# Hybrid trunk layer: the last tile's stash in the context's place, its second pass begun in the scan, outs and gates in separate places, and w_ada issued in turn

## The chip, the cores and the metric

The kernel runs on one core of one Trainium2 chip. The metric is the device time of one execution in microseconds (us), lower is better. The core has five engines with a queue of instructions each: PE (TensorE, matmuls; the loading of its weights is listed as PEld), DVE (VectorE), ACT (ScalarE), POOL (GpSimd) and SP (SyncE, which here only issues DMA transfers). An engine takes its instructions strictly in order.

## The reference

One layer on 2048 latent tokens and 256 context tokens of width 1024, batch 1. The part around the change is the mixer, a gated linear recurrence with 8 heads of 128 in two directions:

```python
m_l = (sc_lat @ w_ada[l] + b_ada[l])[:, None, :]     # sc_lat = silu(c); six vectors of 1024
hl = modulate(rmsnorm(lat, norm_g[l, 0]), sh1, sc1)
q, zf_fwd, zf_bwd, v, g = split(hl @ w_in)
S_t = diag(f_t) S_{t-1} + k_t v_t^T,  o_t = S_t^T q_t     # per head, forward and backward
y = (rmsnorm(o_fwd + o_bwd, g_gain) * silu(g)) @ w_out
lat = lat + g1 * y
hl = modulate(rmsnorm(lat, norm_g[l, 1]), sh2, sc2)
lat = lat + g2 * conv_ffn(hl, w_up, conv_w, conv_b, w_down)
return rmsnorm(lat, final_g)
```

## The kernel before, in words

The 2048 tokens are 16 tiles of 128, numbered 0 to 15 (NT = 16), in two groups of 8 and units of 4. Products are made of operands split in two parts (`split`, L76 to L78: ACT rounds, DVE subtracts), with three matmuls for high-high, high-low and low-high.

**Head (L186 to L230).** The first two of the six modulation vectors come from 16 tiles of `w_ada`, 128x1024 each (512 KB). All 16 transfers are issued first (L199), eight on ACT's queue and eight on SP's; then ACT does the sigmoid (L201), DVE the product (L202), and TensorE 64 matmul passes into `mps` (L208). The x tiles of the first norms are loaded behind (`early_x`).

**Scan (`mixer_scan`, L269 to L736).** For each group and head the projections (L332 to L334) and the forward and backward recurrence in chunks. Work is put on an agenda: `at(clock + n, f)` runs f n ticks later, one tick per step of the projections, and this sets the order of the code. What the backward state from later tiles must still add is kept for a second pass: for each tile, per head, the summed k v products, the decayed q, the outputs o so far and the gates g go to DRAM (`stash`), all but the last head of tile 15, which stays in `late`, inside the tile Sf. In the last head of the second group `out_weight` loads and scales w_out (L634, L635) and splits it into the `wo` places; rows 4 to 7 are held in the context's place (tag cxt) and split after the scan.

**Second pass (`mixer_out`, L877 to L1095).** From tile 15 down to 0: `heads(t)` multiplies the running state Sb with the tile's q (L908), adds o (L912), squares on ACT (L915), updates Sb (L917), sums the squares (L920), makes 1/rms on POOL (L74) and scales o (L925 on DVE, L927 on ACT). `heads_T` transposes o (L937), multiplies with the gate (L939) and splits into ghl (L77, L78). `residual` has 24 matmuls for each half of the row (L948 to L950) and adds to lat (L953). The norm of the tile above follows (`norm_steps`, L955 to L962; `norm2`, transposes at L109), and sums of its transposes are stored for the FFN (L974). The kq and og loads (L889) go over SP; each has two places, for even and odd tiles, and og holds outs and gates in one place that one load fills. The gate product is written over the gates. Code order is `heads` two tiles ahead, `heads_T` one ahead, inside the first `residual`.

The order of instructions on each engine comes from the code's order and a scheduler that works on it; a place of a pool is given again when its last reader is done. Transfers take one of eight semaphore lanes in turn, so that one waits for the eighth before it.

The FFN follows (L1234 and on), untouched but for shifts of time.

## Time and profile before

| what | us |
|---|---|
| median of 3 runs (2834.51 to 2838.2) | 2835.72 |
| the profiled execution | 2833.49 |
| its span | 2831.8 |
| TensorE busy | 2735.7 |
| w_ada's matmuls, start and length | 15.21, 29.49 |
| the scan's last matmul, start | 1270.78 |
| second pass, first matmul | 1280.98 |

The span is the time between the first and the last instruction recorded; the little that is missing to the execution's time lies around it. Rows of a timeline give start, duration, engine, line, operation, output and inputs, and in brackets how long the engine had been idle and what ended this. In a busy row, matmuls are pipelined: their modelled ends lie past the next one's start.

### The profile page before, as it was taken

The page shows a single profiled execution, that of the slowest core. Times are in us where ns is not written, and L with a number is a line of the kernel's source. Part 1 is how long each engine was busy: PE and PEld are TensorE (multiplying, and loading weights), DVE is VectorE, ACT ScalarE, POOL GpSimd, SP SyncE. Part 2 cuts the span into 40 slices and gives each one's busy share as a digit, 9 for nine tenths or more (in the row PEclk, how much of TensorE's full clock was granted, in tenths as well). Part 3 has the DMA queues.
Part 4 walks back from the last instruction along what each step waited for, and adds up shares of the span by engine and source line. Part 5 has one row for each costly group of instructions (what it writes and reads, how often), then busy time and mean ns, then how long its engine had stood idle before and what let it go on. Part 6 is the DMA issues. An engine that isn't in the chain of part 4 may idle for free.

```text
span 2831.8 us, 41982 instructions
## 1 busy us (share of the span) xinstructions
PE 2735.7 (97%) x16072; PEld 2267.8 (80%) x16072; DVE 1978.9 (70%) x2804; ACT 1149.9 (41%) x1910; POOL 563.6 (20%) x882
## 2 busy tenths in 40 slices
PE   6899999999999999998898899999999999999998
PEld 2688888888888888886777788888888888887887
DVE  3555556657565765667787788777878777576887
ACT  4523443333333333334556444444444444333343
POOL 2211111111111111111110343333444332000001
PEclk9899999999999999999999999999999999999999
DMA  5122332224542442226778522226422223987663
GB/s 223 34 68 83 109 112 84 93 60 153 179 127 72 128 125 80 91 76 224 253 276 288 209 90 90 68 81 217 155 89 90 90 71 113 310 305 252 191 201 123
DMA packets 223777, 402.18 MB, mean 142 GB/s; under 512 B 29012, under 2 KB 136404, under 8 KB 217816
## 3 DMA queue, kind: packets, MB, share of 16 engines
q1 hardware_dynamic: 219544, 390.78, 41.6%
q10 hardware_dynamic: 4032, 8.72, 0.8%
q8 instruction: 126, 2.06, 0.3%
q14 instruction: 75, 0.61, 0.1%
HBM read 289.04 MB, written 110.38 MB: 141 GB/s over the span
## 4 chain that ended last, share of the span: by engine, by line
PE 67%; DMA 7%; DVE 6%; issue 1%; ACT 1%; POOL 1%; SPq 0%; DVEq 0%; ACTq 0%; POOLq 0%
PE z L332 8%; PE z L334 8%; PE z L333 7%; PE y L1395 3%; PE y L1393 3%; PE y L1394 3%; PE zc L790 3%; PE zd L790 3%; PE zd L793 3%; PE zc L793 3%; PE zd L792 3%; PE zc L792 3%; PE za L793 3%; PE za L790 3%; PE za L792 3%; PE kv L536 1%
## 5 line engine op out<-in xcount | busy, mean ns | idle before, releaser
L332 PE MATMUL z<-tok,w 128*128 128x512 f32 x1280 | 516.3, 404 | 0.0
L334 PE MATMUL z<-tok,w 128*128 128x512 f32 x1280 | 503.1, 393 | 0.0
L333 PE MATMUL z<-tok,w 128*128 128x512 f32 x1280 | 501.6, 392 | 0.0
L78 DVE TENSOR_TENSOR w<-raw,w 128x512 fp32r<-128x512 f32 (+1 forms) x260 | 239.4, 925 | 144.6 <-ACT w L77 140.7
L334 PEld LDWEIGHTS z<-tok,w 128*128 128x128 f32 x1280 | 241.5, 189 | 51.2
L332 PEld LDWEIGHTS z<-tok,w 128*128 128x128 f32 x1280 | 242.5, 190 | 47.5 <-issue 3.5
L333 PEld LDWEIGHTS z<-tok,w 128*128 128x128 f32 x1280 | 242.1, 189 | 44.7
L77 ACT ACTIVATE w<-raw 128x512 fp32r<-128x512 f32 (+1 forms) x260 | 195.7, 759 | 131.3 <-PE zd L793 77.1
L1395 PE MATMUL y<-wd,ml 128*128 128x512 f32 x600 | 234.0, 390 | 2.6 <-DVE ml L78 2.6
L1393 PE MATMUL y<-wd,mh 128*128 128x512 f32 x600 | 233.7, 389 | 0.7 <-ACT X L1428 0.7
L1394 PE MATMUL y<-wd,mh 128*128 128x512 f32 x600 | 233.5, 389 | 0.0
L386 DVE TENSOR_TENSOR_SCAN S<-F,d 128x528 f32<-128x528 f32 (+1 forms) x80 | 91.6, 1145 | 99.8 <-ACT F L369 99.2
L78 DVE TENSOR_TENSOR w<-s,w 128x512 fp32r<-128x512 f32 x126 | 121.3, 967 | 52.5 <-ACT w L77 51.7
L790 PE MATMUL zc<-rT,w 128*128 128x512 f32 x352 | 137.1, 390 | 1.2 <-DVE uv L1280 1.0
L793 PE MATMUL zc<-rT,w 128*128 128x512 f32 x352 | 136.9, 389 | 0.0
L792 PE MATMUL zc<-rT,w 128*128 128x512 f32 x352 | 136.9, 389 | 0.0
L1395 PEld LDWEIGHTS y<-wd,ml 128*128 128x128 f32 x600 | 112.6, 188 | 27.8 <-DVE ml L78 4.5
L77 ACT ACTIVATE w<-s 128x512 fp32r<-128x512 f32 x126 | 78.2, 627 | 137.3 <-POOL s L846 80.6
L1393 PEld LDWEIGHTS y<-wd,mh 128*128 128x128 f32 x600 | 112.6, 188 | 24.8 <-ACT X L1428 1.2
L1394 PEld LDWEIGHTS y<-wd,mh 128*128 128x128 f32 x600 | 112.6, 188 | 23.3
L790 PE MATMUL za<-rB,w 128*128 128x512 f32 x336 | 130.7, 389 | 0.0
L792 PE MATMUL za<-rB,w 128*128 128x512 f32 x336 | 130.7, 389 | 0.0
(323 smaller groups left out, 6220.1 us busy)
## 6 DMA issues: line engine op xcount, KB each, us to landing
raw<-in_w_up_dram SPq DMA_DIRECT2D x88, 512.0 KB, 4.1
raw<-in_w_in_dram SPq DMA_DIRECT2D x80, 512.0 KB, 3.8
lr<-m SPq DMA_DIRECT2D x49, 512.0 KB, 5.5
m<-r SPq DMA_DIRECT2D x66, 256.0 KB, 4.1
spare<-in_w_ada_dram SPq DMA_DIRECT2D x32, 512.0 KB, 4.9
kq<-stash SPq DMA_DIRECT2D x15, 1024.0 KB, 5.6
og<-stash SPq DMA_DIRECT2D x15, 1024.0 KB, 6.0
u<-in_w_down_dram SPq DMA_DIRECT2D x51, 256.0 KB, 4.0
```

Of the source, the lines that this page charges most:

```text
L77: act.activation(h, src, AF.Copy)
L78: dve.tensor_tensor(l, src, h.bitcast(F32), OP.subtract)
L332: pe.matmul(z, w[:, 0, k], h, start=k == 0, stop=False, skip_group_check=True)
L333: pe.matmul(z, w[:, 0, k], l, start=False, stop=False, skip_group_check=True)
L334: pe.matmul(z, w[:, 1, k], h, start=False, stop=k == KT - 1, skip_group_check=True)
L386: dve.tensor_tensor_scan(flat(S[:, d]), flat(F[:, d]), flat(d1[:, 0:ns]), 0.0, OP.mult, OP.max)
L790: pe.matmul(o, w[:, 0, k], r[:, :, 0, k], start=start and k == 0, stop=False, skip_group_check=True)
L792: pe.matmul(o, w[:, 0, k], r[:, :, 1, k], start=False, stop=False, skip_group_check=True)
L793: pe.matmul(o, w[:, 1, k], r[:, :, 0, k], start=False, stop=k == 3, skip_group_check=True)
L1393: pe.matmul(z, lh, rh, start=start, stop=False, skip_group_check=True)
L1394: pe.matmul(z, lh, rl, start=False, stop=False, skip_group_check=True)
L1395: pe.matmul(z, ll, rh, start=False, stop=stop, skip_group_check=True)
```

## The change

The stash gets the layout [128, 4, 8, 128], one plane each for k v, q, o and g. Three things are done.

**In the head**, the sigmoid and its product stand before the loop over k, and each k issues its two w_ada transfers and its matmuls; the x tiles are issued after k = 3, 4 and 5.

**At the end of the scan**, tile 15's stash for heads 0 to 6 is loaded into the context's place (`load_top`, 12 ticks into the last head), and the last head's four planes are copied there directly. Its head step (`last_heads`) is put beside the last unit's output gate, and its transposes and gate product (`last_turn`) right after the scan, into places of Sf and raw. Rows 4 to 7 of w_out now use the ring of the w_in weights, and all rows are asked for in another order (4 to 7, then 0 to 3, a tick apart). The steps that finish the last head's units come earlier.

**In the second pass**, outs and gates have a place and a load of their own, both issued in `turn` behind the transposes; the gate product is written to PSUM and split from there. `heads(14)` stands in tile 15's first residual half, `heads(13)` behind it, tile 15's `turn` after its second half, the other turns after k = 1 in place of 3, and the load of `conv` after tile 15.

```diff
-        for n, wt in enumerate(wts):
-            (sp if n % 2 else act).dma_start(
-                wt, a["w_ada"][n // 2 * 128:(n // 2 + 1) * 128, n % 2 * D:(n % 2 + 1) * D])
         act.activation(sil, vec[:, V_C:V_C + 16], AF.Sigmoid)
         dve.tensor_tensor(sil, sil, vec[:, V_C:V_C + 16], OP.mult)
-        for t in range(-2, 1):
-            early_x(t)
         for k in range(KT):
             for i in range(2):
+                n = 2 * k + i
+                wt = ada[n // 4][:, n % 4]
+                (sp if i else act).dma_start(
+                    wt, a["w_ada"][k * 128:(k + 1) * 128, i * D:(i + 1) * D])
...
+            if 3 <= k < 6:
+                early_x(k - 5)
...
+        def load_top():
+            tops.append(hq.tile([128, 4, NH, 128], F32, name="top", tag="cxt", bufs=1))
+            sp.dma_start(tops[0][:, :, 0:NH - 1], stash[NT - 1][:, :, 0:NH - 1])
...
+        def last_heads():
+            heads_core(tops[0], tops[0][:, 2], NT - 1,
+                       lambda: ps.tile([128, 4, 128], F32, name="oi", tag=banks.pop(0), bufs=1),
+                       lambda n: gp.tile([128, NH], F32, name=n, tag=n, bufs=1))
...
-            query(1, 14)
-            value(0, (5, 9, 13))
-            if g == 1 and h == NH - 1:
-                value(1, (9, 13, 17))
+            query(1, 13 if last else 14)
+            value(0, (4, 7, 10) if last else (5, 9, 13))
+            if last:
+                value(1, (3, 5, 7))
+                at(clock[0] + 9, last_heads)
                 out_gate(0)
-                for k in range(4):
-                    at(clock[0] + 2 * k, lambda k=k: out_weight(k))
+                weight(4)
+                for n, k in enumerate((4, 5, 6, 7, 0, 1, 2, 3)):
+                    at(clock[0] + n, lambda k=k: out_weight(k))
...
         run(1 << 30)
+        last_turn()
         for k in range(4, KT):
...
-    ogs2 = qp.tile([128, 2, NH, 2, 128], F32, name="og", tag="og", bufs=1)
+    ogs2 = qp.tile([128, 2, 2, NH, 128], F32, name="og", tag="og", bufs=1)
...
-                g = og[:, hs, 1]
-                dve.tensor_tensor(g, tp, g, OP.mult)
-                split(gh[:, hs], gl[:, hs], g)
+            dve.tensor_tensor(tp, tp, g_[:, hs], OP.mult)
+            split(gh[:, hs], gl[:, hs], tp)
...
         def turn():
-            gs.append(heads_T(t - 1, ogs.pop(0)))
+            gs.append(heads_T(t - 1))
+            if t > 1:
+                load_stash(3, 1, t - 2)
+            if t > 2:
+                load_stash(2, 1, t - 3)
...
-            residual(0, lat, *g, between=turn if 0 < t < NT - 1 else None)
             if t == NT - 1:
-                turn()
-            if t > 2:
-                gts[t - 3] = load_stash(1, t - 3)
+                residual(0, lat, *g, between={3: lambda: heads(t - 1)})
+                heads(t - 2)
+            else:
+                residual(0, lat, *g, between={1: turn} if t else {})
```

What stands in order on three engines, before and after. First ACT at the program's start (wada are the tiles of w_ada, sil the sigmoid, x_ the first token tiles). Before:

```order
L199 DMA wada<-in_w_ada_dram 128x1024 x8
L201 ACT_TABLE_LOAD
L201 ACTIVATE sil<-vec 128x16
L97 ACTIVATE junk,ss<-x_168 128x1024
L100 ACTIVATE x_168<-x_168,rs 128x1024
```

After:

```order
L202 DMA wada<-in_w_ada_dram 128x1024 x2
L196 ACT_TABLE_LOAD
L196 ACTIVATE sil<-vec 128x16
L202 DMA wada<-in_w_ada_dram 128x1024 x4
L97 ACTIVATE junk,ss<-x_176 128x1024
L202 DMA wada<-in_w_ada_dram 128x1024
L100 ACTIVATE x_176<-x_176,rs 128x1024
```

The sigmoid now has two transfers ahead of it in place of eight, and the others stand between it and the norms' squares.

Next DVE where the scan ends and the second pass begins (wo are the split parts of w_out, raw, spare and wraw its rows; L374, L414 are the scan's last gate). Before:

```order
L78 TENSOR_TENSOR wo<-raw,wo 128x1024
L78 TENSOR_TENSOR wo<-spare,wo 128x1024
L78 TENSOR_TENSOR wo<-raw,wo 128x1024
L374 TENSOR_TENSOR g<-z,g 128x512
L78 TENSOR_TENSOR wo<-spare,wo 128x1024 x3
L917 SCALAR_TENSOR_TENSOR Sb<-Sb,decb,kq 128x128 x5
L912 TENSOR_TENSOR og<-og,oi 128x4x128
L917 SCALAR_TENSOR_TENSOR Sb<-Sb,decb,kq 128x128
L912 TENSOR_TENSOR og<-og,oi 128x4x128
L917 SCALAR_TENSOR_TENSOR Sb<-Sb,decb,kq 128x128 x2
L920 TENSOR_REDUCE ss_11971<-oi 128x4 x2
```

After, from the sums of tile 15's squares on (L289 to L294 are the lines that stood at L920 to L925, L304 stood at L939, L677 at L635; top is tile 15's stash):

```order
L289 TENSOR_REDUCE ss_11826<-oi 128x4 x2
L78 TENSOR_TENSOR wo<-raw,wo 128x1024
L73 TENSOR_SCALAR rs_11827<-ss_11826 128x8
L677 SCALAR_TENSOR_TENSOR raw<-raw,vec,g_11234 128x1024
L294 TENSOR_TENSOR top<-top,rs_11827 128x512
L414 TENSOR_TENSOR g<-z,g 128x512
L78 TENSOR_TENSOR wo<-wraw,wo 128x1024
L78 TENSOR_TENSOR wo<-raw,wo 128x1024
L677 SCALAR_TENSOR_TENSOR raw<-raw,vec,g_11234 128x1024
L304 TENSOR_TENSOR tp<-tp,top 128x512 x2
L78 TENSOR_TENSOR wo<-raw,wo 128x1024
L78 TENSOR_TENSOR gl<-tp,gh 128x512 x2
```

Before, all pieces of w_out are split before the first instruction of tile 15; now the head step of tile 15 stands ahead of most of them, and its gate product (L304) and split (gl) among them. On TensorE the eight matmuls of tile 15's head step now have the last 21 matmuls of the scan's gate behind them, then come its transposes, 29 matmuls of the residual, and the eight of tile 14's head step, with the 19 that are left of tile 15's two halves behind them.

Last SP inside the second pass, from the kq load of one tile on (stash_79 is tile 15's, stash_73 tile 9's). Before, from an og load to the second next store of lat:

```order
L889 DMA og<-stash_75 128x2048
L1059 DMA lat_94<-lat 128x1024
L974 DMA rhs1T_11914<-w 128x1024
L889 DMA kq<-stash_73 128x2048
L1019 DMA lat<-in_x_dram 128x1024
L889 DMA og<-stash_74 128x2048
L1059 DMA lat_93<-lat 128x1024
```

After:

```order
L1044 DMA lat<-in_x_dram 128x1024
L949 DMA kq<-stash_73 128x2048
L949 DMA og<-stash_74 128x1024
L1091 DMA lat_93<-lat 128x1024
L949 DMA og<-stash_73 128x1024
L1003 DMA rhs1T_11968<-w 128x1024
```

One og load of 128x2048 has become two of 128x1024: gates (those of tile 10, stash_74) come behind the kq of tile 9, and outs (those of tile 9, stash_73) behind the store of lat.

## The prediction

> **What bounds the kernel now.** First the page: its span, and how busy each engine is.

> ```profile
> span 2831.8 us, 41982 instructions
> ...
> PE 2735.7 (97%) x16072; PEld 2267.8 (80%) x16072; DVE 1978.9 (70%) x2804; ACT 1149.9 (41%) x1910; POOL 563.6 (20%) x882
> ```

> TensorE is the bound; no matmul is removed by this change, so all that can go is its idle time, or its time at a low clock. The profiled execution took 2833.49 us for a span of 2831.8; the median of the three runs shown is 2835.72, 2.2 above it. I make the sum against 2833.5 and add 2.2 at the end. A measurement of this kernel can tell about 0.2% (5.7 us) from no change.

> Next the waits of TensorE (us in total, times, longest), to see what the idle time is:

> ```profile
> PE mps L208 <- DVE sil L202: 15.2, 1, 15.2
> PE y L948 <- DVE lat L953: 13.4, 7, 4.6
> ...
> PE tp L109 <- DVE xn L962: 8.5, 7, 2.1
> ```

> Then the busy time by stretch (PE, PEld, DVE, ACT, POOL; then the granted clock, DMA share, GB/s):

> ```profile
> 200.00:1263.00 1063.00, 1059.63 (x8255) 898.72 (x8254) 675.54 (x976) 357.67 (x608) 162.59 (x398) 1.00 0.33 103
> ...
> 1322.00:1516.30 194.30, 177.29 (x962) 148.86 (x961) 153.16 (x324) 109.95 (x256) 25.98 (x24) 1.00 0.73 256
> ```

> The scan is full (1059.6 of 1063), so nothing is to be won inside it. The reader should see three holes, and each has one part of the change on it: the first 15.2 us, the handover from scan to second pass (rows below), and the second pass (17.0 us of 194.3).

> **Head: w_ada issued in turn.** The timeline of the first microseconds (start, duration, engine, line):

> ```profile
> 0.81 12.60 ACTq L199 DMA_DIRECT2D wada<-in_w_ada_dram  x8
> ...
> 4.26 0.17 DVE L243 TENSOR_TENSOR lbw<-vec 128x16 f32<-128x16 f32 x1 [4.26 <-DMA vec<-in_vecs_dram]
> ...
> 13.44 1.28 ACT L201 ACT_TABLE_LOAD   x1 [13.44 <-DMA wada<-in_w_ada_dram]
> 14.73 0.22 ACT L201 ACTIVATE sil<-vec 128x16 f32<-128x16 f32 x1
> 14.98 0.18 DVE L202 TENSOR_TENSOR sil<-sil,vec 128x16 f32<-128x16 f32 x1 [3.46 <-ACT sil L201]
> ...
> 15.21 29.49 PE L208 MATMUL mps<-wada,sil 128*2 128x512 f32 x64 [15.21 <-DVE sil L202]
> ```

> The sigmoid needs only vec, which is there at 4.26, but it stands on ACT behind eight DMA issues that take until 13.44. Afterwards two issues stand ahead of it. Its table load needs no data, so it can run before 4.26; sigmoid 0.22, product 0.18 and two hops of 0.05 to 0.25 put TensorE's start at about 5.0, or at 5.9 if the table load waits for vec: I take 5.3. Then the weights must keep up:

> ```profile
> GB/s 0 159 365 385 396 412 421 412 418 412 412 407 415 410 404 412 407 423 410 421 407 407 112 0 243 265 246 251 44 0 11 0 0 0 0 0 0 96 377 333
> ```

> The forty slices of 0 to 60 us show some 410 GB/s, so a 512 KB tile each 1.28 us, 2.56 us for the two of one k; TensorE spends 29.49/8 = 3.7 us on a k. It isn't starved. The DMA burst, x tiles and first raws included, ends in slice 22 (33 us), before the matmuls would (5.3 + 29.5 = 34.8). So the whole start moves by 15.2 − 5.3 = **9.9 us** (8 to 10.5); what follows to 200 us hangs on these sums and moves along.

> **Handover.** TensorE's timeline, from the scan's last matmul to the first transposes of norm2:

> ```profile
> 1270.78 0.39 PE L562 MATMUL o<-v,at 128*128 128x128 f32 x2
> 1280.98 3.78 PE L908 MATMUL oi<-Sb,kq 128*128 128x128 f32 x16 [9.80 <-DMA kq<-stash]
> 1288.55 3.56 PE L908 MATMUL oi<-Sb,kq 128*128 128x128 f32 x16 [3.80 <-DVE ss L920]
> ...
> 1294.55 0.50 PE L948 MATMUL y<-wo,ghl 128*128 128x512 f32 x1 [1.22 <-ACT ghl L77]
> ...
> 1308.49 1.95 PE L908 MATMUL oi<-Sb,kq 128*128 128x128 f32 x16
> 1310.19 0.48 PE L948 MATMUL y<-wo,ghl 128*128 128x512 f32 x1
> ...
> 1313.01 1.04 PE L937 MATMUL tp<-ident,og 128*128 128x128 f32 x8
> ...
> 1321.87 0.39 PE L950 MATMUL y<-wo,ghl 128*128 128x512 f32 x1
> 1322.10 1.03 PE L109 MATMUL tp<-ident,xn 128*128 128x128 f32 x8
> ```

> From 1271.17 to 1322.10 are 50.9 us. In them lie four head groups (from 1308.49 to the next start at 1310.19: 1.7 each, since a modelled end overlaps the next start by 0.25), three transpose groups (1.04, so 0.8) and 96 matmuls of the residual (the last at 1321.87, 0.23 before the next): 31.3 us. So 19.6 are lost: the gaps of 9.80, 3.80 and 1.22, and half speed around them.

> The change takes away the wait for the load of tile 15, but puts its head group in front of the last 21 gate matmuls (4.8 us) and tile 15's whole readout behind them, on DVE. Prices of the operations, by groups (busy, mean ns, idle before) and then from DVE's timeline:

> ```profile
> L912 DVE TENSOR_TENSOR og<-og,oi 128x512 f32<-128x512 f32 x32 | 21.3, 683 | 24.5 <-DMA og<-stash 24.5
> ...
> L920 DVE TENSOR_REDUCE ss<-oi 128x4 f32<-128x512 f32 x32 | 20.5, 682 | 0.0
> ...
> L939 DVE TENSOR_TENSOR og<-tp,og 128x512 f32<-128x512 f32 x32 | 21.8, 684 | 3.6 <-PE tp L937 3.6
> ...
> L77 ACT ACTIVATE ghl<-og 128x512 fp32r<-128x512 f32 x32 | 19.2, 621 | 9.6 <-DVE og L939 9.6
> ...
> L74 POOL TENSOR_TENSOR rs<-rs,mhalf 128x8 f32<-128x8 f32 x16 | 26.4, 1650 | 88.1 <-DVE rs L73 88.1
> ```

> ```profile
> 1270.53 1.29 DVE L635 SCALAR_TENSOR_TENSOR raw<-raw,vec,g 128x1024 f32<-128x1024 f32 x1 [1.32 <-DMA raw<-in_w_out_dram]
> 1271.73 1.22 DVE L78 TENSOR_TENSOR wo<-raw,wo 128x1024 fp32r<-128x1024 f32 x1
> ...
> 1292.10 1.13 DVE L917 SCALAR_TENSOR_TENSOR Sb<-Sb,decb,kq 128x128 f32<-128x128 f32 x4
> ```

> By the order on DVE: two adds 1.4, eight Sb updates 2.1 (four take 1.13), two sums 1.3, a wo split 1.2, the power on POOL 1.7 with its hops 0.4, the scaling 0.7: 8.8 from the head group to the transposes, less 4.8 of cover: **4.0 idle**. Between transposes and the first residual matmul stand a last piece of the scan's gate 0.7, two wo splits 2.4, a scaling of raw 1.3, the gate multiplication 0.7 and ACT's rounding 0.6: 5.7, less 0.8 beside the transposes and 0.7 because DVE's instructions begin up to 0.1 before the one ahead ends (the split at 1271.73 behind the scaling that lasts to 1271.82): **4.2**, then 0.8 for gl. Half clock behind that is 2.5 (the tail below shows such a stretch). Head group 14 has the same chain without the split and with some overlap, 7.2, over 19 matmuls (4.3): 2.9. The two lat additions, the next gate product and rounding: 2.7; half clock after these gaps 2.5. Sum 19.6 against 19.6 lost: **gain 0**. Bounds: 7 better if the weight splits slip behind the chain, 6 worse if raw for k = 3 lands late, since its scaling stands in this chain:

> ```profile
> raw<-in_w_out_dram SPq DMA_DIRECT2D x2, 512.0 KB, 5.1
> ```

> It can be issued only when the split ahead frees its place, and the work between is about 5.9 us: enough cover for 5.1 and an issue, nothing to spare.

> How long a gap brings half speed these rows bound: behind the tail's 4.59 (below) the matmuls come at half rate, and in front of the gap of 3.80 the head groups were slow already (3.78 against 1.95 later).

> [...]

> **Second pass, tiles 13 to 2.** Six pairs of tiles run from 1322.10 to the row of 1516.31 below: 194.2/6 = 32.4 us a pair, with 177.29/6 = 29.5 of matmuls. What delays them starts at DVE, as its waits in 1296 to 1560 us show:

> ```profile
> DVE og L912 <- DMA og<-stash: 22.5, 9, 3.6
> DVE og L925 <- POOL rs L74: 18.5, 15, 1.5
> ```

> The timeline of one tile (its transposes, then the load into its place), and SP's waits, show what holds the loads:

> ```profile
> 1395.57 1.03 PE L937 MATMUL tp<-ident,og 128*128 128x128 f32 x8
> ...
> 1407.85 0.32 SPq L889 DMA_DIRECT2D og<-stash  x1
> ```

> ```profile
> SPq L889 <- DVE ghl L78: 78.2, 14, 7.9
> ```

> DVE waits up to 3.6 us for outs of the next tile, since one load brings outs and gates into one place, and SP can't issue it before the last ghl split of the tile whose place it takes has read the product there. In order behind that wait stand xn and lat, and TensorE waits for those. With places apart, outs come free with the transposes, and the product goes to PSUM, so gates come free one multiplication later, not after two splits (L939 reads PSUM at 684 ns, L912 and L920 cost the same; the splits of a product in PSUM are taken at that price). By the order the outs' load is issued right after those transposes: near 1396.6 in place of 1407.85, 11 us earlier, where it comes 3.6 late at most. DVE then has 153.16/6 = 25.5 of work a pair and 2 x 1.23 of waits for POOL: 28 to 29, under TensorE's 29.5. I take 29.9 a pair: 6 x 2.5 = **15 us** (6 to 17: the upper end is all of TensorE's idle, the lower leaves two waits in three). The extra DMA issue per tile on SP (0.3 us) is covered by SP's waits of the row above.

> **Tail.**

> ```profile
> 1516.31 1.06 PE L109 MATMUL tp<-ident,xn 128*128 128x128 f32 x8 [0.67 <-DVE xn L962]
> 1521.96 0.77 PE L948 MATMUL y<-wo,ghl 128*128 128x512 f32 x1 [4.59 <-DVE lat L953]
> ...
> 1527.22 1.27 PE L937 MATMUL tp<-ident,og 128*128 128x128 f32 x8
> ```

> The gap of 4.59 is the same DVE chain, with nothing else for TensorE; the 12 matmuls after it take 5.26 us to 1527.22, 0.44 each where 0.23 is full speed: 2.5 lost. With DVE some 2 us ahead, as without a wait of 3.6 at most behind it, the gap is 2.4 and the clock stays up: 2.2 + 2.5, taken as **4** (0 to 7).

> **Sum.** −9.9 + 0 − 15 − 4 = −29; 2833.5 − 29 = 2804.5; with 2.2 it is **2807**.

> **Rivals.** A: the handover really closes: TensorE finds the chain of tile 15 nearly done, since the wo splits slip behind it or beside the scan. For it: DVE has 4.2 us of splits in the chain that nothing there needs. Against: they stand in DVE's order. It saves up to 13 of the 19.6 more: 2794.

> B: the second pass only trades its wait: DVE has just 0.8 us of slack a pair, and rhs stores, lat and kq loads share the 0.73 of DMA. Then head and a little remain: 2833.5 − 9.9 − 1 + 2.2 = 2825. The edit would be done, and not do what it says for the outs.

> C, slower: SP is one queue in order, now with four loads a tile, and an outs load that waits for transposes stands ahead of the kq load and of the rhs stores whose buffers DVE needs. If that makes each of 14 tiles 1.3 us later: 2833.5 + 18.2 − 9.9 + 2.2 = 2844. It decides from 9.9/14 = 0.7 us a tile. Against it: the 78.2 us that SP already waits for the splits, most of which go.

> D: the clock falls in both new gaps of the handover. Eight transposes and up to 12 matmuls more go at half rate, 0.9 to 2.5 more: about 2809. [...]

> **Chances.** Forecast 0.58, A 0.14, B 0.17, D 0.06, C 0.05. The range takes the forecast with its unknowns (handover, pairs), A and D and the nearer side of B: 2792 to 2823. Faster by over 0.2% (under 2830) are all but C and the far side of B: 0.92; within 0.03; slower 0.05.

> **What would show it.** Head: the mps group starts near 5 and lasts 29.5; later than 7, and the sigmoid still waited. Handover: no wait for kq; instead two waits of about 4 us, for the scaled outs and for the gate product; a wait of DVE for raw means the load was late. Second pass: the outs' wait for the stash falls from 22.5 to a few us, and the starts of the norm2 transposes lie under 30.5 apart; if they lie at 32, B holds. Tail: the 4.59 halves. Wrong would be above all a DVE whose waits move to rhs buffers or kq at the same length.

## The result, and the profile after

The changed kernel takes 2798.89 us (median of 4 runs, 2796.79 to 2800.06) against 2835.11 before (4 runs, 2834.23 to 2838.2): a ratio of 0.9869, 95% interval 0.9852 to 0.9887, so 36 us faster where 29 were forecast. The page of its profiled execution:

```profile
span 2797.0 us, 42007 instructions
...
PE 2732.9 (98%) x16072; PEld 2269.1 (81%) x16072; DVE 1977.5 (71%) x2804; ACT 1147.7 (41%) x1908; POOL 571.9 (20%) x882
```

The span is 34.8 us shorter. The waits of TensorE, as shown of before (us in total, times, longest):

```profile
PE mps L205 <- DVE sil L197: 5.2, 1, 5.2
PE y L977 <- ACT gh L77: 3.8, 1, 3.8
...
PE tp L303 <- ACT top L296: 3.5, 1, 3.5
...
PE tp L303 <- DVE og L294: 3.2, 2, 1.8
...
PE y L977 <- ACT ghl L77: 1.8, 1, 1.8
...
PE tp L109 <- DVE xn L991: 0.5, 1, 0.5
```

The wait for lat (13.4 us in 7 places), that for kq (9.8) and that for xn in the second pass are gone; new are those of 3.5, 3.8 and three of under 2 in the handover. The twelve tiles of the second pass, by stretch (PE, PEld, DVE, ACT, POOL, clock, DMA share, GB/s):

```profile
1312.40:1486.20 173.80, 173.80 (x961) 149.45 (x960) 154.89 (x329) 108.53 (x258) 34.08 (x24) 1.00 0.84 293
```

TensorE has no idle time left in them. The table sets the two profiled executions side by side; each row is a difference of starts or ends in the timelines.

| stretch of TensorE | before | after | forecast | measured |
|---|---|---|---|---|
| start to the last gate or scan matmul's end | 1271.17 | 1262.03, with 1.7 of tile 15's head step in it | −9.9 | −10.8 |
| from there to the first norm2 transposes | 50.9 | 50.4, without that head step | 0 | +1.2 |
| twelve tiles | 194.2 | 173.8 | −15 | −20.4 |
| from there to the first zd matmul of the FFN | 56.6 | 49.2 | −4 | −7.5 |
| rest (FFN) | 1258.8 | 1261.6 | 0 | +2.8 |

The rest isn't the change's doing as far as the runs show: over the profiled executions told of below it lies between 1257.6 and 1263.3, and the changed kernel run once more had 1257.6.

### The profile page after: what moved, and what is told of

The parts are those of the page before. It is cut to its first block, busy times and chain, and to the rows that moved or that the text cites. A ratio compares the mean times of both kernels' runs of the same rounds, so it can differ in the third digit from the quotient of the medians.

```text
span 2797.0 us, 42007 instructions
## 1 busy us (share of the span) xinstructions
PE 2732.9 (98%) x16072; PEld 2269.1 (81%) x16072; DVE 1977.5 (71%) x2804; ACT 1147.7 (41%) x1908; POOL 571.9 (20%) x882
## 5 line engine op out<-in xcount | busy, mean ns | idle before, releaser
L374 PE MATMUL z<-tok,w 128*128 128x512 f32 x1280 | 502.5, 393 | 0.0
L78 DVE TENSOR_TENSOR w<-raw,w 128x512 fp32r<-128x512 f32 (+1 forms) x260 | 239.6, 925 | 146.8 <-ACT w L77 142.8
L374 PEld LDWEIGHTS z<-tok,w 128*128 128x128 f32 x1280 | 241.3, 189 | 51.2
L77 ACT ACTIVATE w<-raw 128x512 fp32r<-128x512 f32 (+1 forms) x260 | 196.1, 760 | 134.0 <-PE zd L857 77.4
L78 DVE TENSOR_TENSOR w<-s,w 128x512 fp32r<-128x512 f32 x126 | 121.0, 965 | 54.5 <-ACT w L77 53.7
L77 ACT ACTIVATE w<-s 128x512 fp32r<-128x512 f32 x126 | 78.3, 628 | 138.8 <-POOL s L910 82.2
L459 POOL COPY TX<-S 128x4 f32<-128x4 f32 x32 | 25.1, 784 | 529.0 <-DVE S L426 529.0
L854 PE MATMUL za<-rB,w 128*128 128x512 f32 x336 | 130.7, 389 | 0.0
## 6 DMA issues: line engine op xcount, KB each, us to landing
raw<-in_w_up_dram SPq DMA_DIRECT2D x88, 512.0 KB, 3.9
raw<-in_w_in_dram SPq DMA_DIRECT2D x80, 512.0 KB, 3.8
lr<-m SPq DMA_DIRECT2D x49, 512.0 KB, 5.7
spare<-in_w_ada_dram SPq DMA_DIRECT2D x32, 512.0 KB, 4.5
og<-stash SPq DMA_DIRECT2D x28, 512.0 KB, 5.2
```

The source lines that it names most:

```text
L77: act.activation(h, src, AF.Copy)
L78: dve.tensor_tensor(l, src, h.bitcast(F32), OP.subtract)
L374: pe.matmul(z, w[:, 1, k], h, start=False, stop=k == KT - 1, skip_group_check=True)
L854: pe.matmul(o, w[:, 0, k], r[:, :, 0, k], start=start and k == 0, stop=False, skip_group_check=True)
```

## Experiments

Times are medians; "before" is the kernel before, measured beside them on the same chip, and each ratio is to it. Where two variants are compared by stage, it is by TensorE's timeline of one profiled execution each.

### The head alone, and the sigmoid alone

`head_only` is the kernel before with the head's hunk of the change. `sig_first` only moves two lines:

```diff
+        act.activation(sil, vec[:, V_C:V_C + 16], AF.Sigmoid)
+        dve.tensor_tensor(sil, sil, vec[:, V_C:V_C + 16], OP.mult)
         for n, wt in enumerate(wts):
             (sp if n % 2 else act).dma_start(
...
-        act.activation(sil, vec[:, V_C:V_C + 16], AF.Sigmoid)
-        dve.tensor_tensor(sil, sil, vec[:, V_C:V_C + 16], OP.mult)
```

> The kernel before with only the head of the change: sigmoid ahead of the transfers, w_ada issued k by k, x tiles behind k = 3 to 5. Theory (the head's 10.4 us, 44.70 to 34.27 at the end of w_ada's matmuls, go through to the end): 2835.1 - 10.4 = 2824.7, between 2823 and 2827; the second pass keeps its 13.4 us of waits for lat. Rival (what is won at the start is lost again in the first 200 us, where TensorE also waits for x tiles and the first projections' weights): over 2830.

> The kernel before with only the two lines of the sigmoid and its product put ahead of the 16 issues; all 16 are still issued in one loop, the x tiles behind them. Theory (what counts is that ACT does the sigmoid before its eight issues; the issues in turn add nothing, since TensorE needs 3.7 us for each k and the transfers 2.56): w_ada's matmuls start at 5 to 6 us, and the time is that of the run with the whole head, within 1 us: 2824 to 2826. Rival (the turn-by-turn issue matters, because ACT's issues stand behind the sigmoid and the x tiles come late): the matmuls stall or the first norms wait, and 3 us or more of the 10.4 are missing.

`head_only`: 2826.49 against 2836.67, ratio 0.9964 (0.9952 to 0.9975). `sig_first`: 2828.91, ratio 0.9972 (0.9961 to 0.9983). The starts of w_ada's matmuls, first in `head_only` and then in `sig_first`:

```profile
4.78 29.71 PE L206 MATMUL mps<-wada,sil 128*2 128x512 f32 x64 [4.78 <-DVE sil L198]
```

```profile
4.79 29.00 PE L208 MATMUL mps<-wada,sil 128*2 128x512 f32 x64 [4.79 <-DMA wada<-in_w_ada_dram]
...
35.42 1.27 PE L217 MATMUL mt<-ident,m 2*128 2x2 f32 x12 [1.62 <-ACT m L214]
```

They start alike; at the end of the scan `head_only` stands at 1260.9 and `sig_first` at 1260.4. So the head's 10 us go through, and they come from the place of the sigmoid ahead of ACT's issues. What the issue in turn adds is at most the 1.62 of the last row (ACT's work on the x tiles begins at 25.45 us there and at 16.66 in `head_only`), and that is made up again. `sig_first` as a whole came 2.9 above its bound; the 2.4 between the medians lie within both intervals, and within what the FFN differs from one execution to the next.

### The second pass: which of its edits

Four kernels undo parts of it in the changed kernel. `one_load` fills outs and gates with one load in `turn`; `two_load_sbuf` writes the product over the gates; `one_load_sbuf` does both; `turn_k3` moves the turn.

```diff
 one_load
-        load_stash(2, 1, NT - 3)
+        load_stash(2, 2, NT - 3)
...
-            if t > 1:
-                load_stash(3, 1, t - 2)
             if t > 2:
-                load_stash(2, 1, t - 3)
+                load_stash(2, 2, t - 3)
 two_load_sbuf
-            dve.tensor_tensor(tp, tp, g_[:, hs], OP.mult)
-            split(gh[:, hs], gl[:, hs], tp)
+            g = g_[:, hs]
+            dve.tensor_tensor(g, tp, g, OP.mult)
+            split(gh[:, hs], gl[:, hs], g)
 turn_k3
-                residual(0, lat, *g, between={1: turn} if t else {})
+                residual(0, lat, *g, between={3: turn} if t else {})
```

A fifth, `before_psum`, puts one of them into the kernel before:

```diff
-                dve.tensor_tensor(g, tp, g, OP.mult)
-                split(gh[:, hs], gl[:, hs], g)
+                dve.tensor_tensor(tp, tp, g, OP.mult)
+                split(gh[:, hs], gl[:, hs], tp)
```

> The changed kernel, but outs and gates of a tile come again with one load of 1 MB, issued in turn; so it must wait for the gate product (two multiplications) of the tile whose place it takes, no longer for its transposes alone. The product still goes to PSUM. Theory (the separate places are what counts: the product stands some 8 to 11 us behind the transposes in the changed kernel's profile, at 1397.2 and 1399.8 against 1388.8, so the outs would land about 5 us late): DVE's waits for the outs' load come back with 2 us or more a tile and TensorE's waits for lat and xn with them; 12 to 24 us slower than the changed kernel: 2811 to 2823. Rival (what counts is that the product left the gates' place, so that a load needn't wait for the splits): within 2 us of the changed kernel, 2797 to 2801.

> The changed kernel, but the gate product is written over the gates again and split from there; outs and gates keep separate places and loads. Theory (separate places count): the gates' load waits for the splits, 2 us later, and is needed only a tile later; within 1.5 us of the changed kernel: 2797.5 to 2800.5. Rival (the product in PSUM counts): SP, held up by that load, brings kq and outs later too; waits come back and the time is 8 us or more above, 2807 to 2820.

> The changed kernel, but the turn (transposes, gate product and the two loads) stands after k = 3 of the residual's first half, as before, not after k = 1: six matmuls or 1.4 us later. Theory (separate places count, with slack: the outs' load is issued 11 us before the addition that needs it and takes about 6): within 1.5 us of the changed kernel, 2797.5 to 2800.5. Rival (the earlier turn is what keeps DVE ahead): 1.4 us a tile come back in 13 tiles, up to 18 us slower.

> The changed kernel with both parts of the new places undone: one load of 1 MB for outs and gates, and the gate product written over the gates and split from there, so that the load waits for the splits. Each part alone, undone, cost the second pass about 7 us or less (the twelve tiles took 177.2 and 174.3 us in place of 173.8, the stretch behind them 3.7 and 0.9 more). Theory (either part is enough, since the load then comes some 2 us or more earlier; only both undone bring back the wait): the twelve tiles take 185 to 195 us again, the time is 2815 to 2825. Rival (the new order of head step, turn and loads on SP is what counts, and the places are a trifle): within 8 us of the changed kernel, 2799 to 2807.

> The kernel before with one edit: the gate product goes to PSUM (over the transposes) and is split from there, so that the load of outs and gates waits for the product and not for the splits. Theory (that wait alone starts the chain of waits of the second pass): the twelve tiles fall from 194.2 to 176 to 182 us and the gap of 4.59 shrinks; 12 to 20 us faster than before: 2816 to 2824. Rival (the old order of loads and turns keeps the wait): within 4 us of the kernel before.

| kernel | us | ratio to before (95%) | twelve tiles | to zd |
|---|---|---|---|---|
| one_load | 2802.7 | 0.9889 (0.9871 to 0.9907) | 177.2 | 52.9 |
| two_load_sbuf | 2801.35 | 0.9875 (0.9860 to 0.9891) | 174.3 | 50.1 |
| turn_k3 | 2795.72 | 0.9861 (0.9847 to 0.9876) | 173.8 | 50.0 |
| one_load_sbuf | 2826.97 | 0.9960 (0.9946 to 0.9974) | 197.0 | 56.4 |
| before_psum | 2820.64 | 0.9940 (0.9925 to 0.9954) | 178.7 | 55.4 |

My theory of `one_load` fell: it expected 12 to 24 us of loss, and the stage lost 3.4 and the tail 3.7; its rival's bound of 2801 was missed by 1.7. That of `two_load_sbuf` held in its mechanism (0.5 and 0.9), with a median 0.85 above its bound. So one part undone costs 7.1 or 1.4 us in these two stages; both undone bring back all that the second pass had won. DVE's waits for the load of outs between 1290 and 1530 us, in this order for `one_load`, `one_load_sbuf` and `before_psum`:

```profile
DVE og L281 <- DMA og<-stash: 4.8, 5, 1.3
```

```profile
DVE og L281 <- DMA og<-stash: 25.9, 12, 4.1
```

```profile
DVE og L912 <- DMA og<-stash: 6.2, 4, 2.3
```

In the changed kernel and in `two_load_sbuf` this row is absent. With both undone (the time a little beyond its bound, 197.0 where 195 was the most) it is as large as before the change (22.5), with the new order of head steps, turns and loads in place, so that order isn't what wins. The rival that makes the product in PSUM count holds as far as the load is one; with two loads it hardly matters. In `before_psum`, two changed lines give 17 of the 28 us, as its theory expected (178.7 us for the twelve tiles, a median inside its bounds).

### The handover

`heads_after` asks for tile 15's head step after the scan; `warm` puts 27 matmuls that nothing reads into the two gaps (work that the reference doesn't need); `wraw6b` loads rows 2 and 3 of w_out into the ring too:

```diff
 heads_after
-                at(clock[0] + 9, last_heads)
...
         run(1 << 30)
+        last_heads()
         last_turn()
 warm
...
+                    for i in range(count):
+                        pe.matmul(z, wo0[:, 0, 0:128], wo0[:, 0, 0:512], start=i == 0, stop=i == count - 1)
 wraw6b
-            if k < 4:
+            if k < 2:
                 raw = rawp.tile([128, D], F32, name="raw", tag="raw")
...
-                for n, k in enumerate((4, 5, 6, 7, 0, 1, 2, 3)):
+                for n, k in enumerate((0, 1, 2, 3, 4, 5, 6, 7)):
```

> The changed kernel, but the head step of tile 15 is asked for after the scan, not beside the last gate (its stash is still loaded early into the context's place). Theory (the 21 gate matmuls cover 4.8 us of the chain on DVE and POOL): that cover is lost, while splits of w_out move ahead of the chain and leave it; 2 to 5 us slower, 2801 to 2804. Rival (DVE's sum of splits and readout is the bound from 1254 to 1277 us, in whatever order): within 1 us of the changed kernel.

> The changed kernel with 27 matmuls more that nothing reads (128x512, from a finished part of w_out into a free PSUM bank): 15 ahead of tile 15's transposes, 12 behind them, in the two gaps of 3.55 and 3.81 us. They are work that the reference doesn't need. Theory (the clock falls in a gap of 3.55 us, as the transposes' 2.21 us in place of 1.03 show): the transposes take 1.1 and the 13 matmuls behind the second gap 0.23 each; 1.2 + 2.6 less what DVE's chain then ends later: 2 to 4 us faster, 2795 to 2797. Rival (the half speed after those gaps isn't the clock, or DVE's splits bound the stretch anyway): no gain, or up to 3 us slower if the extra matmuls come in the way.

> The changed kernel, but rows 2 and 3 of w_out are loaded into the weights' ring like rows 4 to 7, so that their two scalings (1.28 us each) stand on DVE before tile 15's head step, not inside its chain; rows are asked for in the order 0 to 7. Theory (DVE's chain sets both gaps): the gap ahead of tile 15's transposes falls from 3.55 to about 2.5 and that ahead of the residual from 3.81 to 1.5 or less, with less time at half clock; 4 to 8 us faster, 2791 to 2795. Rival (the splits of rows 4 to 7 and the readout fill DVE in any order, or the scan is held up by the earlier scalings): within 1.5 us of the changed kernel.

Against 2835.8: `heads_after` 2802.06, ratio 0.9880 (0.9863 to 0.9896); `warm` 2799.99, 0.9872 (0.9857 to 0.9887); `wraw6b` 2796.01, 0.9854 (0.9839 to 0.9869). The stretch from the scan's last matmul to the first norm2 transposes is 53.6, 49.9 and 44.6 us. First the changed kernel's TensorE, then its DVE and POOL in this chain:

```profile
1255.27 1.95 PE L277 MATMUL oi<-Sb,top 128*128 128x128 f32 x16
...
1265.57 2.21 PE L303 MATMUL tp<-ident,top 128*128 128x128 f32 x8 [3.55 <-ACT top L296]
1271.59 0.80 PE L977 MATMUL y<-wo,gh 128*128 128x512 f32 x1 [3.81 <-ACT gh L77]
...
1277.83 0.44 PE L978 MATMUL y<-wo,gh 128*128 128x512 f32 x1
...
1281.56 1.95 PE L277 MATMUL oi<-Sb,kq 128*128 128x128 f32 x16
...
1289.58 1.10 PE L303 MATMUL tp<-ident,og 128*128 128x128 f32 x8 [1.76 <-DVE og L294]
1292.44 0.79 PE L977 MATMUL y<-wo,ghl 128*128 128x512 f32 x1 [1.76 <-ACT ghl L77]
...
1294.32 3.62 PE L277 MATMUL oi<-Sb,kq 128*128 128x128 f32 x16
```

```profile
1262.22 0.16 DVE L73 TENSOR_SCALAR rs<-ss 128x8 f32<-128x8 f32 x1
1262.29 1.28 DVE L677 SCALAR_TENSOR_TENSOR raw<-raw,vec,g 128x1024 f32<-128x1024 f32 x1
1265.12 0.69 DVE L294 TENSOR_TENSOR top<-top,rs 128x512 f32<-128x512 f32 x1 [1.55 <-POOL rs L74]
...
1268.69 1.27 DVE L677 SCALAR_TENSOR_TENSOR raw<-raw,vec,g 128x1024 f32<-128x1024 f32 x1
1269.88 1.29 DVE L304 TENSOR_TENSOR tp<-tp,top 128x512 f32<-128x512 f32 x2
```

```profile
1262.46 2.62 POOL L74 TENSOR_TENSOR rs<-rs,mhalf 128x8 f32<-128x8 f32 x1 [27.35 <-DVE rs L73]
```

In `wraw6b` without the two scalings:

```profile
1262.81 2.07 PE L303 MATMUL tp<-ident,top 128*128 128x128 f32 x8 [3.48 <-ACT top L296]
1267.11 0.80 PE L977 MATMUL y<-wo,gh 128*128 128x512 f32 x1 [2.23 <-ACT gh L77]
```

The second gap falls from 3.81 to 2.23, the first hardly: POOL's power ends it, and beside that power DVE now has a split of 1.22 in place of the scaling of 1.28; the power takes 2.56 in place of 2.62. The first half of that expectation missed, the second came near (2.23 where 1.5 or less was expected). The stretch is 5.8 us shorter than in the changed kernel's first profile, but part of that is the clock (below), and the profiled execution, of 2788.61, is 7.2 us faster than the next of its four. The median is 1.0 above the expected range, and its interval overlaps the changed kernel's, so that a gain isn't shown. In `heads_after` one gap of 12.43 replaces the first one, and the stage, which there holds the head step's 1.7, is 1.5 us longer than the changed kernel's 52.1. The changed kernel's own executions differ by 1.3 there (below), so the cover is small if it is there at all.

`warm` tells what the clock does and what it's worth:

```profile
1267.06 1.06 PE L303 MATMUL tp<-ident,top 128*128 128x128 f32 x8 [0.54 <-DVE top L294]
1272.69 0.50 PE L984 MATMUL y<-wo,gh 128*128 128x512 f32 x1 [1.80 <-ACT gh L77]
```

With the first gap filled the transposes take 1.06 and not 2.21: the 2.21 was half speed. But 1.4 us later the matmuls were at half speed again, TensorE waited 3.57 us for tile 14's outs where it had waited 1.76, and no time was won. The theory was right on the clock and wrong on its worth; the rival (the DVE chain bounds the stretch) held.

### The best two edits together, and the changed kernel again

`wraw6_k3` is `wraw6b` with the edit of `turn_k3`; `after_again` is the changed kernel.

> The changed kernel with both edits that did best: rows 2 and 3 of w_out in the weights' ring, in the order 0 to 7, and the turn after k = 3. Theory (the first shortens the handover by about 5 us; the second does nothing by itself, and what it seemed to bring was the clock's luck in the handover): 3 to 6 us faster than the changed kernel run beside it. Rival (both count): 6 to 9 us faster.

> The changed kernel once more, beside the others of this call. Theory (how long half speed lasts behind the gaps of the handover differs from one execution to the next): the same instruction order and about the same gaps (3.5, 3.8, 1.8, 1.8), but the stretch from the scan's last matmul to the first norm2 transposes is not 50.4 us as in the first profile but up to 4 us shorter; second pass and tail within 0.3 us of 173.8 and 49.2. Rival (an execution is like another): that stretch within 0.5 us of 50.4.

Against 2837.83: `after_again` 2795.48, ratio 0.9853 (0.9838 to 0.9868); `wraw6_k3` 2792.75, ratio 0.9843 (0.9828 to 0.9858). That is 2.7 us between them where 3 to 6 were expected, with intervals that overlap: a version that is better by a measurable amount isn't shown. `after_again` did the stretch to norm2 in 49.1 us, 1.3 shorter than the first time, with the same gaps (3.54, 3.82, 1.76, 1.76); second pass 173.8 and tail 49.2 as expected. The same order with those gaps, in `turn_k3`:

```profile
1289.28 1.09 PE L303 MATMUL tp<-ident,og 128*128 128x128 f32 x8 [1.77 <-DVE og L294]
1292.14 0.50 PE L977 MATMUL y<-wo,ghl 128*128 128x512 f32 x1 [1.76 <-ACT ghl L77]
```

There the matmul behind the fourth gap, and the head step at 1293.17 (1.95), run at full speed; in `after_again` they take 0.80 and 3.48, in the changed kernel's first profile 0.79 and 3.62. That is why the profiled execution of `turn_k3` took 46.9 for the stretch. Its median lay under its expected range, but the changed kernel's second median of 2795.48 does so too: no sign of a gain by the later turn. `wraw6b` was spared too (44.6), `wraw6_k3` was not (48.5).

## Why the prediction was right, point by point

The measured 2798.89 lies in the range of 2792 to 2823. Two of the forecast's four terms left their own bounds, though (the second pass with 20.4 over 17, the tail with 7.5 over 7), and the handover came out by two misses that cancel; that the sum stayed inside is in part luck, since the range was also held open for rival A's 2794.

- **Head, −9.9: right.** TensorE starts at 5.16 (5.3 was taken), w_ada's matmuls aren't starved (29.11 us long in place of 29.49), and the start's gain stays. `head_only` measures 10.2 by itself. Only the credit was too wide: the sigmoid's place does it.
- **Handover, 0: right in size, in part by luck.** Forecast were gaps of 4.0, 4.2, 0.8, 2.9 and 2.7; the profile has 3.55, 3.81, 0.15, 1.76 and 1.76, then 1.44. That is 2.1 less in sum; what is lost beside the gaps, half speed above all, is 8.3 where 5.0 was counted. Rival D's mechanism (the clock falls in the first gap too) came true, with 2.21 us for the transposes in place of 1.03, and the clock falls once more after the pair of 1.76, which nothing forecast. The prediction took the length of a gap for what decides. The profile of before has two gaps from full speed that are shorter than the tail's 4.59 and near each other, of 2.27 at 92.07 us, which kept full speed, and of 2.74 at 69.97, which lost it 0.2 us later. What else went with the clock is in the last section. The raw for k = 3 wasn't late. Nothing measures this part alone undone; its +1.2 and, in the second execution, −0.1 are what is left between scan and norm2.
- **Second pass, −15 (6 to 17): the mechanism was right, the size too small.** It gave 20.4, more than the upper end, which I had called all of TensorE's idle. That step failed: recorded idle isn't all that a gap costs. Ahead of each gap the overlap with the next instruction is lost, so that what stands there counts as busy in full: the 177.3 busy us of before became 173.8 for the same instructions. Two rows of before show it:

```profile
1389.08 1.95 PE L908 MATMUL oi<-Sb,kq 128*128 128x128 f32 x16
1392.60 0.47 PE L948 MATMUL y<-wo,ghl 128*128 128x512 f32 x1 [1.57 <-DVE lat L953]
```

The head step ahead of the gap counts for its 1.95, where the one at 1308.49, with no gap behind it, has the next matmul 1.70 after its start: 0.25 more than its share. A residual matmul ahead of a gap counts for its 0.39 in place of 0.23, 0.16 more. Six gaps of the first kind and seven of the second make 2.6 of the 3.5. And I took 29.9 us a pair where TensorE's own 29.0 was reached, since DVE (154.9/6 = 25.8 a pair) and its waits for POOL left the slack that was worked out.
- **What in the second pass wins it: half right.** The prediction put the places apart and the product in PSUM down as one answer. The runs show that either is nearly enough (177.2 and 174.3 us) and that only both undone bring the wait back. Its times of the load were right: in the changed kernel outs are issued at 1389.96, 1.1 behind the start of their tile's transposes:

```profile
1388.84 1.04 PE L303 MATMUL tp<-ident,og 128*128 128x128 f32 x8
```

```profile
1389.96 0.32 SPq L949 DMA_DIRECT2D og<-stash  x1
```

- **Tail, −4 (0 to 7): too small, and just beyond its bound; the same mechanism.** The gap of 4.59 was forecast to halve and vanished, with the half speed behind it: 7.5. That the clock stays up through a gap of 2.4, as the forecast has it, was the author's estimate: no run shows it for this place, and of the gaps of 2.27 and 2.74 in the profile of before only the first kept full speed.
- **Rivals.** B (the wait only changes its name) and C (SP's queue) are refuted by the 173.8 us without idle time. A didn't come: gaps of 3.55 and 3.81 stand where it had the handover closed, and `wraw6b` shortens only the second, to 2.23.

## What to carry to other kernels

Look for what releases a buffer that a transfer waits for: here two edits each moved the last reader a little earlier, and either sufficed to take most of a 22.5 us wait out of a loop. Put a short instruction ahead of a run of DMA issues on its queue, since the issues hold the engine (eight of them for 12.6 us here, two of them alone for 0.90 in the changed kernel). When a stall goes, count the broken overlap as well as the recorded idle (0.16 or 0.25 us a gap here), and keep for the place that follows a gap the time at half speed (the 12 matmuls behind the 4.59 took 5.26 us, 0.44 each in place of 0.23).

## What the runs showed of the hardware

Half speed went with more than the length of a gap. A gap of 3.5 us brought it in each of five profiles (changed kernel twice, `turn_k3`, `wraw6b`, `wraw6_k3`: transposes of 2.07 to 2.21 us where `warm` has 1.06). Two gaps of 1.76 with eight transposes between them brought it in three of the same five (changed kernel twice, `wraw6_k3`: 3.48 to 3.62 us for the next head step) and not in two (`turn_k3`, `wraw6b`: 1.95), and behind the second gap of the handover it lasted from 3.6 us (`wraw6b`) to 6.3 (`wraw6_k3`).

```profile
87.26:90.68 3.42, 2.54 (x12) 1.77 (x10) 3.37 (x5) 0.82 (x2) 2.22 (x3) 1.00 0.00 0
90.68:94.09 3.41, 2.02 (x11) 1.77 (x12) 1.44 (x5) 1.75 (x2) 0.15 (x1) 1.00 0.00 0
100.92:104.33 3.41, 1.55 (x9) 1.01 (x8) 1.92 (x6) 1.52 (x2) 1.03 (x2) 1.00 0.00 0
104.33:107.74 3.41, 3.41 (x12) 2.73 (x10) 3.26 (x8) 0.75 (x2) 0.00 (x0) 0.50 0.00 0
```

The longer gap kept full speed and the shorter one lost it. With the two profiles cut in this way from 19.00 and from 8.17 us on, where their records begin, 1603 stretches are at full speed: the 15 in which TensorE was idle for 1.86 us or more were all followed by half speed, and of the 1588 with 1.72 or less only one was. In the changed kernel's first profile the stretch before the fall behind the pair of 1.76 (1288.17 to 1291.58) held 2.32 us idle, with parts of both gaps.

With the same gaps, half speed behind the second gap of the handover ended at different times in the changed kernel's two executions of 50.4 and 49.1 us: 6.3 us behind it in the first (1277.93, by the clock's record), 4.6 in the second (about 1276.5, where its matmuls begin 0.23 apart again in place of 0.43).

POOL's power over 128x8 took 2.56 to 2.62 us in the handover of seven profiles with the new head step (changed kernel twice, `two_load_sbuf`, `heads_after`, `warm`, `wraw6b`, `wraw6_k3`), and 1.64 to 1.67 at its other places in the handovers. In each of the seven, DVE had begun an instruction on rows of 1024 (a scaling or a split, 1.22 to 1.28) 0.17 or 0.18 us before the power, and the power ended 1.51 or 1.52 us after that instruction did. That DVE's instruction is the cause is not shown by any run.
